# Zero-padded whole-array matmuls for attention and norms, and a reordered first stage, in a one-core encoder step

## The chip, the core and the metric

The kernel runs on one core of a Trainium2 chip. The metric is device time in microseconds (us): the median of three runs, and beside it one profiled execution, whose trace all rows below come from. The engines are called as the profile calls them: PE multiplies matrices (PEld is its weight load), DVE, ACT and POOL work elementwise, SP only issues transfers; ACT and POOL issue some too.

## The reference, cut to what matters

One layer for T = 320 positions (256 of a prompt, 64 of a running stream), model width 2048, everything in float32:

```python
z = rmsnorm(x) @ w_in                       # 2048 -> 3328: q 1024, k 128, v 128, gate input 2048
q, k = rmsnorm(q, q_g), rmsnorm(k, k_g)     # 16 query heads of 64, 2 key/value heads of 64
s = q @ k.T / 8 + bias                      # chunk of 64 queries against up to 192 keys
w = exp(s - m) / (sum(exp(s - m)) + exp(sink - m))
attn = w @ v
sgu = u * (W_s @ rmsnorm(v2) + b)           # u, v2 = gelu of the gate input; blocks of 128 positions
x = x + concat(rmsnorm(attn), rmsnorm(sgu)) @ w_out            # 2048 x 2048
y = x + square(relu(rmsnorm(x) @ w_up)) @ w_down               # 2048 x 8192 and back
```

## The kernel before, in words

Everything is held transposed: channels on the 128 partitions, the 320 positions along the free axis. The four large products run through `products` (L98): a weight block of 4 x 128 rows and 256 columns is loaded by SP into `w_raw` (the first stage into `w_first`), ACT rounds it into `w_hi` (L115), DVE takes the rest into `w_lo` (L116), and PE runs three passes per 128 x 128 piece, XH·w_hi, XL·w_hi and XH·w_lo (L125), each one instruction of 128x320. There are 8160 such instructions, called products from here on. `w_hi` and `w_lo` have two buffers each.

Between them stand the small float32 matmuls, each of which is two PE instructions (a transpose is one). `rstd_rows` (L136) sums squares over partitions into row form, three matmuls, the third for 64 positions; `spread` (L150) brings them back over 128 partitions. The first stage (L183) makes k, v and the first 256 columns of q, 192 products; `load_x` brings in x as it goes. Then the k norm is applied, `kq` holds keys times the gain, and `ksw` the same with the two key heads' partitions exchanged by two transfers from POOL. `attend(unit)` (L283) works on 64 queries and half of the heads' partitions, `hs`: four score matmuls of 64 rows into `s_ps` (L290), bias, softmax, four or eight transposes through `ident` (L321), and value matmuls with 64 output columns (L329). The gate group is mixed in L384 and L385, the latter with 64 rows. `bias` is built at the start: `tab` times `oneh` (L199) makes a row, which goes to DRAM as `b_dram` (L204) and comes back in 16 transfers (L212).

The order on each engine is set by a scheduler that simulates the program when it is built; each engine then works strictly in that order. The 192nd product ends the first stage; products are numbered along PE's order. PE's attention work stands between the 338th and 974th product.

Of the kernel before, what the change touches and what calls it, by code (L numbers as in the profile page):

```python
# [15 lines left out]
T = 320  # L16
TT = [(0, 128), (128, 128), (256, 64)]
# [11 lines left out]
def hymba_step_kernel(ctx: ExitStack, tc: tile.TileContext, i, o):  # L29
# [32 lines left out]
    nc.scalar.dma_start(out=xT[:, 0:1], in_=xv[:, 0:1])  # L62
# [29 lines left out]

    def chunks(n, first):
        if first:
            return [(0, 1), (1, 1), (2, 2)] + [(a, 4) for a in range(4, n, 4)]
        return [(a, 4) for a in range(0, n, 4)]

    def products(w, k0, nk, jobs, rh, rl, first=None, deep=None):  # L98
# [3 lines left out]
        for a, n in chunks(nk, first is not None):  # L102
# [4 lines left out]
            for j, (c0, ps) in enumerate(jobs):  # L107
# [6 lines left out]
                nc.sync.dma_start(out=raw[:, :n], in_=wv[:, k0 + a:k0 + a + n, c0:c0 + 256])  # L114
# [6 lines left out]
                for (k, g), (w_, r_, x) in [(kg, p_) for p_ in passes for kg in kgs] if first is not None else \  # L121
                        [(kg, p_) for kg in kgs for p_ in passes]:
                    kk = a + k
                    out = ps[g][:, 0:T] if isinstance(ps, list) else ps[:, g, 0:T]
                    nc.tensor.matmul(out=out, lhsT=w_[:, k, g * P:(g + 1) * P], rhs=r_(kk),  # L125
                                     start=(kk == 0 and x == 0), stop=(kk == nk - 1 and x == 2))
# [9 lines left out]
    def rstd_rows(sq, weight, eps, h=1):  # L136

        st = misc()
        for t, (t0, n) in enumerate(TT):
            nc.tensor.matmul(out=st[0:n, t * h:t * h + h], lhsT=sq[:, t0:t0 + n], rhs=weight, start=True, stop=True)  # L140
        r = sm.tile([P, 3 * h], F32, name="r_rows", tag="r_rows")
        nc.vector.memset(r[HD:P, 2 * h:3 * h], 1.0)
        nc.vector.tensor_scalar(out=r[:, 0:2 * h], in0=st[:, 0:2 * h], scalar1=eps, scalar2=None, op0=ALU.add)
        nc.vector.tensor_scalar(out=r[0:HD, 2 * h:3 * h], in0=st[0:HD, 2 * h:3 * h], scalar1=eps, scalar2=None,
                                op0=ALU.add)
# [30 lines left out]
    kq = at.tile([P, 448], F32, name="kq", bufs=1)  # L176
    ksw = at.tile([P, 448], F32, name="ksw", bufs=1)
# [43 lines left out]
    ssq = sm.tile([P, T], F32, name="ssq", tag="ssq", bufs=2)  # L221
    nc.vector.tensor_tensor(out=ssq, in0=ssq2[:, 0], in1=ssq2[:, 1], op=ALU.add)
# [7 lines left out]
    sq = sm.tile([P, T], F32, name="ksq", tag="w1", bufs=3)  # L230
    nc.scalar.activation(out=sq, in_=zk, func=AF.Square)
# [5 lines left out]
    for t, (t0, n) in enumerate(TT):  # L237
        nc.tensor.matmul(out=bc[:, t0:t0 + n], lhsT=rkx[0:n, t], rhs=ident[0:n, 0:n], start=True, stop=True)
    for dst, c in ((kn[:, 0:256], slice(0, 256)), (kn[:, 384:448], slice(256, 320))):
        nc.vector.scalar_tensor_tensor(out=dst, in0=zk[:, c], scalar=g_k, in1=bc[:, c], op0=ALU.mult, op1=ALU.mult)  # L240
    nc.vector.tensor_scalar(out=kq, in0=kn, scalar1=g_q, scalar2=None, op0=ALU.mult)
    nc.gpsimd.dma_start(out=ksw[0:HD], in_=kq[HD:P])
    nc.gpsimd.dma_start(out=ksw[HD:P], in_=kq[0:HD])
# [14 lines left out]
    for g in range(4):  # L258
# [16 lines left out]

    blocks = [
        (0, 0, 64, 128, None, vn[0]),
        (64, 0, 128, 64, vn[0], None),
        (128, 0, 192, 0, vn[0], vn[2]),
        (192, 64, 192, 0, vn[1], vn[3]),  # L280
        (256, 256, 192, 0, vC, vn[4]),
    ]
    def attend(unit):  # L283
        q0, k0, nk, b0, va, vb = blocks[unit // 2]
        p = unit % 2
        hs = slice(p * HD, (p + 1) * HD)
        s_ps = ps_sc.tile([P, 4, 256], F32, name="s_ps", tag="s_ps")
# [4 lines left out]
        s = at.tile([P, 4, 192], F32, name="s", tag="s", bufs=2)  # L292
        for j in range(4):
            c = 2 * (unit // 2) + p
            nc.vector.scalar_tensor_tensor(out=s[:, j, 0:nk], in0=s_ps[:, j, 0:nk], scalar=rq[:, j, c:c + 1],
                                           in1=bias[:, p, j, b0:b0 + nk], op0=ALU.mult, op1=ALU.add)
        m = at.tile([P, 4], F32, name="m", tag="m")
        nc.vector.tensor_reduce(out=m, in_=s[:, :, 0:nk], axis=AX.X, op=ALU.max)
        sk = sinks[:, 4 * p:4 * p + 4]
        nc.vector.tensor_tensor(out=m, in0=m, in1=sk, op=ALU.max)  # L300
        nm = at.tile([P, 4], F32, name="nm", tag="nm")
        nc.vector.tensor_scalar(out=nm, in0=m, scalar1=-1.0, scalar2=None, op0=ALU.mult)
        es = at.tile([P, 4], F32, name="es", tag="es")
        nc.vector.tensor_tensor(out=es, in0=sk, in1=m, op=ALU.subtract)
        nc.scalar.activation(out=es, in_=es, func=AF.Exp)
        den = at.tile([P, 4], F32, name="den", tag="den")
        for j in range(4):
            nc.scalar.activation(out=s[:, j, 0:nk], in_=s[:, j, 0:nk], func=AF.Exp, bias=nm[:, j:j + 1],
                                 accum_out=den[:, j:j + 1])
        nc.vector.tensor_tensor(out=den, in0=den, in1=es, op=ALU.add)  # L310
        nc.vector.reciprocal(out=den, in_=den)
        nc.gpsimd.tensor_tensor(out=s[:, :, 0:nk], in0=s[:, :, 0:nk],
                                in1=den[:, :, None].to_broadcast([P, 4, nk]), op=ALU.mult)
        parts = []
        c = 0
        for part, v, n in (("a", va, 128), ("b", vb, 64)):
            if v is None:
                continue
            pt_ps = misc()
            for j in range(4):  # L320
                nc.tensor.transpose(out=pt_ps[0:n, j * P:(j + 1) * P], in_=s[:, j, c:c + n], identity=ident)  # L321
            pt = at.tile([P, 512], F32, name="pt" + part, tag="pt" + part, bufs=1)
            nc.vector.tensor_copy(out=pt[0:n], in_=pt_ps[0:n])
            parts.append((pt, v, n))
            c += n
        for kv in range(2):
            o_ps = misc()
            for x, (pt, v, n) in enumerate(parts):
                nc.tensor.matmul(out=o_ps[hs, 0:256], lhsT=v[0:n, kv * HD:(kv + 1) * HD],  # L329
                                 rhs=pt[0:n, kv * 256:(kv + 1) * 256],  # L330
                                 start=(x == 0), stop=(x == len(parts) - 1))
            nc.scalar.activation(out=ao[hs, 4 * kv:4 * kv + 4, q0:q0 + 64],
# [190 lines left out]
```

## Time and profile before

| | |
|---|---|
| median of 3 runs | 1282.88 us (1282.8 to 1282.99) |
| profiled execution | 1281.25 us, span 1279.4 us |
| PE busy | 1272.5 us of the span (99%) |
| PEld, DVE, ACT, POOL busy | 1248.2, 635.2, 492.8, 101.4 us |
| DMA engines, mean rate over the span | 146 GB/s |

The span reaches from the first to the last instruction; the rest of the profiled time lies outside it. A matmul's end is modelled and includes its way through the array, so successive matmuls overlap in the trace; the distance between their starts is what PE spends on one.

### The profile page before, as it was taken

Reading aid. Unit: us, or ns where it says so; the run is one execution under the profiler, and the core shown is the slowest. Engines: PE = TensorE matmul, PEld = TensorE weight load, DVE = VectorE, ACT = ScalarE, POOL = GpSimd, SP = SyncE. Lnnn points to the kernel's source line nnn. Section 1 sums busy time; section 2 is a strip of 40 time slices with the busy share of each in tenths; the row PEclk is TensorE's granted clock in tenths of the full one; section 3 lists DMA queues with packets and bytes.
Section 4 is the critical chain, followed back from the end, with each engine's and each line's share of the span. In section 5 each row is a group of like instructions: output and inputs, shape, how many; then the busy total and the mean of one; then the engine's idle time right before and its main releaser. Section 6 shows DMA issues by size and latency. Waiting matters only on the chain.

```text
span 1279.4 us, 20199 instructions
## 1 busy us (share of the span) xinstructions
PE 1272.5 (99%) x8559; PEld 1248.2 (98%) x8559; DVE 635.2 (50%) x740; ACT 492.8 (39%) x644; POOL 101.4 (8%) x89
## 2 busy tenths in 40 slices
PE   8999999999999999999999999999999999999998
PEld 8999878999999999999999999999999999999998
DVE  7436765665774444343444444344443444444333
ACT  7325556432553433333334322233433323343222
POOL 0123335220230000000000000000000000000000
PEclk9999999999999999999999999999999999999999
DMA  9543323554454444445554444544444455544550
GB/s 301 150 128 99 99 83 100 175 162 149 149 150 147 149 148 149 149 150 149 153 152 154 149 149 149 149 149 149 149 151 152 149 153 151 150 148 159 169 169 32
DMA packets 186459, 187.79 MB, mean 147 GB/s; under 512 B 6400, under 2 KB 185904, under 8 KB 186368
## 3 DMA queue, kind: packets, MB, share of 16 engines
q1 hardware_dynamic: 185504, 185.17, 46.8%
q8 instruction: 67, 1.10, 0.4%
q0 software_dynamic: 432, 0.97, 0.3%
q10 hardware_dynamic: 432, 0.36, 0.1%
q14 instruction: 24, 0.20, 0.0%
HBM read 182.91 MB, written 3.32 MB: 146 GB/s over the span
## 4 chain that ended last, share of the span: by engine, by line
PE 99%; DMA 0%; ACT 0%; issue 0%; DVE 0%; POOL 0%; DVEq 0%; POOLq 0%; ACTq 0%
PE acc L125 92%; PE misc L329 1%; PE misc L125 1%; PE s_ps L290 1%; PE q_ps L125 1%; PE misc L321 1%; PE misc L269 0%; DMA tab<-in_table 0%; PE misc L384 0%; PE misc L140 0%; PE misc L154 0%; PE misc L385 0%; PE misc L376 0%; ACT sq L219 0%; PE misc L199 0%
## 5 line engine op out<-in xcount | busy, mean ns | idle before, releaser
L116 DVE TENSOR_TENSOR w_lo<-w_raw,w_hi 128x1024 fp32r<-128x1024 f32 x332 | 413.9, 1247 | 455.9 <-ACT w_hi L115 438.2
L115 ACT ACTIVATE w_hi<-w_raw 128x1024 fp32r<-128x1024 f32 x332 | 352.1, 1061 | 733.9 <-PE acc L125 684.9
L125 PE MATMUL acc<-H2H,w_lo 128*128 128x320 f32 x1024 | 316.6, 309 | 0.0
L125 PE MATMUL acc<-H2L,w_hi 128*128 128x320 f32 x1024 | 316.4, 309 | 0.0
L125 PE MATMUL acc<-H2H,w_hi 128*128 128x320 f32 x1024 | 316.4, 309 | 0.0
L125 PE MATMUL acc<-FH,w_hi 128*128 128x320 f32 x992 | 306.5, 309 | 0.0
L125 PE MATMUL acc<-FL,w_hi 128*128 128x320 f32 x992 | 306.5, 309 | 0.0
L125 PE MATMUL acc<-FH,w_lo 128*128 128x320 f32 x992 | 306.5, 309 | 0.0
L125 PEld LDWEIGHTS acc<-H2H,w_lo 128*128 128x128 f32 x1024 | 192.2, 188 | 0.1
L125 PEld LDWEIGHTS acc<-H2H,w_hi 128*128 128x128 f32 x1024 | 192.2, 188 | 0.0
L125 PEld LDWEIGHTS acc<-H2L,w_hi 128*128 128x128 f32 x1024 | 192.2, 188 | 0.0
L125 PEld LDWEIGHTS acc<-FH,w_hi 128*128 128x128 f32 x992 | 186.2, 188 | 0.0
L125 PEld LDWEIGHTS acc<-FL,w_hi 128*128 128x128 f32 x992 | 186.2, 188 | 0.0
L125 PEld LDWEIGHTS acc<-FH,w_lo 128*128 128x128 f32 x992 | 186.2, 188 | 0.0
L125 PE MATMUL acc<-XH,w_lo 128*128 128x320 f32 x384 | 117.8, 318 | 0.0
L125 PE MATMUL acc<-XH,w_hi 128*128 128x320 f32 x384 | 117.3, 317 | 0.2 <-ACT w_hi L115 0.2
L125 PE MATMUL acc<-XL,w_hi 128*128 128x320 f32 x384 | 116.1, 313 | 0.0
L125 PEld LDWEIGHTS acc<-XH,w_lo 128*128 128x128 f32 x384 | 71.5, 189 | 4.3 <-issue 3.1
L125 PEld LDWEIGHTS acc<-XH,w_hi 128*128 128x128 f32 x384 | 71.5, 189 | 3.9 <-issue 2.1
L125 PEld LDWEIGHTS acc<-XL,w_hi 128*128 128x128 f32 x384 | 71.6, 189 | 1.6 <-issue 1.4
L440 DVE SCALAR_TENSOR_TENSOR tf<-acc,r 128x640 f32<-128x640 f32 x32 | 26.4, 825 | 43.6 <-PE acc L125 43.6
L454 DVE TENSOR_TENSOR xT<-xT,acc 128x640 f32<-128x640 f32 x31 | 25.5, 821 | 41.8 <-PE acc L125 41.8
(173 smaller groups left out, 1033.8 us busy)
## 6 DMA issues: line engine op xcount, KB each, us to landing
w_raw<-in_w_up SPq DMA_DIRECT2D x128, 512.0 KB
w_raw<-in_w_down SPq DMA_DIRECT2D x128, 512.0 KB
w_raw<-in_w_in SPq DMA_DIRECT2D x44, 512.0 KB
w_raw<-in_w_out SPq DMA_DIRECT2D x32, 512.0 KB
w_first<-in_w_in SPq DMA_DIRECT2D x6, 512.0 KB
out_yT<-xT SPq DMA_DIRECT2D x7, 320.0 KB
xT<-in_xT SPq DMA_DIRECT2D x3, 640.0 KB
bias<-b_dram SPq DMA_DIRECT2D x16, 48.0 KB
```

The lines of the kernel that those rows point to most:

```text
L115: nc.scalar.activation(out=hi[:, :n], in_=raw[:, :n], func=AF.Copy)
L116: nc.vector.tensor_tensor(out=lo[:, :n], in0=raw[:, :n], in1=hi[:, :n].bitcast(F32), op=ALU.subtract)
L125: nc.tensor.matmul(out=out, lhsT=w_[:, k, g * P:(g + 1) * P], rhs=r_(kk), start=(kk == 0 and x == 0), stop=(kk == nk - 1 and x == 2))
L290: nc.tensor.matmul(out=s_ps[:, j, 0:nk], lhsT=qT[hs, q0 // 64, 2 * j:2 * j + 2].rearrange("p a t -> p (a t)"), rhs=keys[hs, k0:k0 + nk], s ...
L321: nc.tensor.transpose(out=pt_ps[0:n, j * P:(j + 1) * P], in_=s[:, j, c:c + n], identity=ident)
L329: nc.tensor.matmul(out=o_ps[hs, 0:256], lhsT=v[0:n, kv * HD:(kv + 1) * HD], rhs=pt[0:n, kv * 256:(kv + 1) * 256], start=(x == 0), stop=(x ...
L440: nc.vector.scalar_tensor_tensor(out=t, in0=ps[:, :, 0:T], scalar=0.0, in1=r2[:, None, :].to_broadcast([P, 2, T]), op0=ALU.max, op1=ALU.mult)
L454: nc.vector.tensor_tensor(out=xT[:, a:a + n], in0=xT[:, a:a + n], in1=p, op=ALU.add)
```

## The change

What the parts of the diff do:

- The table product L199 (L221 after) is ordered behind the last product of the first stage (`issue_after`), and the 16 `bias` transfers go from SP's queue to POOL's.
- x's first block moves from ACT's queue to the head of SP's, and all weight and x loads on SP are chained in program order.
- Scores: keys lie in `kz`, 128 rows of which 64 are zero, once for each half; one matmul of all 128 rows gives both halves' scores side by side. A unit is now 64 queries and one key head.
- Values lie in `vz` between two blocks of 64 zero columns, so that a slice of 128 columns puts one half's result on its partitions and adds zero on the others. Keys are cut 96 + 96 where they were 128 + 64.
- Row sums run over 384 positions, the last 64 zero; `spread`, `rkx` and L385 take all 128 rows.

```diff
-    nc.scalar.dma_start(out=xT[:, 0:1], in_=xv[:, 0:1])
...
+    def load(out, in_):
+        with tc.issue_after(loads[-1].ins) if loads else nullcontext():
+            loads.append(nc.sync.dma_start(out=out, in_=in_))
...
-        for t, (t0, n) in enumerate(TT):
-            nc.tensor.matmul(out=st[0:n, t * h:t * h + h], lhsT=sq[:, t0:t0 + n], rhs=weight, start=True, stop=True)
+        for t in range(3):
+            nc.tensor.matmul(out=st[:, t * h:t * h + h], lhsT=sq[:, t * P:(t + 1) * P], rhs=weight, start=True, stop=True)
...
-            nc.tensor.matmul(out=bc[:, t0:t0 + n], lhsT=rs[0:n, t:t + 1].to_broadcast([n, P]),
-                             rhs=ident[0:n, 0:n], start=True, stop=True)
+            nc.tensor.matmul(out=bc[:, t0:t0 + n], lhsT=rs[:, t:t + 1].to_broadcast([P, P]),
+                             rhs=ident[:, 0:n], start=True, stop=True)
...
-    nc.tensor.matmul(out=b_ps[0:16, 0:255], lhsT=tab, rhs=oneh, start=True, stop=True)
+    with tc.issue_after(mm.ins):
+        nc.tensor.matmul(out=b_ps[0:16, 0:255], lhsT=tab, rhs=oneh, start=True, stop=True)
...
-                nc.sync.dma_start(out=bias[hh * HD:(hh + 1) * HD, p, j], in_=src)
+                nc.gpsimd.dma_start(out=bias[hh * HD:(hh + 1) * HD, p, j], in_=src)
...
-        (192, 64, 192, 0, vn[1], vn[3]),
+        (192, 64, 192, 0, [(vn[64], 96), (vn[160], 96)]),
...
-        for j in range(4):
-            keys = kq if j // 2 == p else ksw
-            nc.tensor.matmul(out=s_ps[:, j, 0:nk], lhsT=qT[hs, q0 // 64, 2 * j:2 * j + 2].rearrange("p a t -> p (a t)"),
-                             rhs=keys[hs, k0:k0 + nk], start=True, stop=True)
+        for j in range(2):
+            a = 2 * (2 * kv + j)
+            nc.tensor.matmul(out=s_ps[:, j, 0:2 * nk].rearrange("x (p k) -> x p k", p=2),
+                             lhsT=qT[:, blk_, a:a + 2].rearrange("p a t -> p (a t)"),
+                             rhs=kz[:, kv, :, k0:k0 + nk], start=True, stop=True)
...
-                nc.tensor.matmul(out=o_ps[hs, 0:256], lhsT=v[0:n, kv * HD:(kv + 1) * HD],
-                                 rhs=pt[0:n, kv * 256:(kv + 1) * 256],
+                nc.tensor.matmul(out=o_ps[:, 0:256], lhsT=v[0:n, kv, HD - p * HD:3 * HD - p * HD],
+                                 rhs=pt[0:n, p * 256:(p + 1) * 256],
...
-        nc.tensor.matmul(out=sp_ps[:, 256:T], lhsT=vnat_s[:, cs], rhs=wsT[0:HD, g, 0:HD], start=True, stop=True)
+        nc.tensor.matmul(out=sp_ps[:, 256:T], lhsT=vnat_s[:, cs], rhs=wsT[:, g, 0:HD], start=True, stop=True)
```

**How rows move.** First the start of PE's order (`acc` is the sum for k and v, `q_ps` that for q), before and then after:

```order
L78 MATMUL misc<-idle 128x256 x3
L199 MATMUL misc<-oneh,tab 16x255
L125 MATMUL acc<-XH,w_hi 128x320 x2
L125 MATMUL q_ps<-XH,w_hi 128x320 x2
L125 MATMUL acc<-XL,w_hi 128x320 x2
```
```order
L78 MATMUL misc<-idle 128x256 x3
L132 MATMUL acc<-XH,w_hi 128x320 x2
L132 MATMUL acc<-XL,w_hi 128x320 x2
L132 MATMUL acc<-XH,w_lo 128x320 x2
L132 MATMUL q_ps<-XH,w_hi 128x320 x2
```

The table product is gone from the front (it follows the 192nd product), and k and v take their three passes before q begins. Next ACT at the same place, from the first block of x up to the first weight block of 4 x 128 rows (128x1024), before and after; 128x256 and 128x512 are the blocks of rows 0 to 1 and 2 to 3:

```order
L162 ACTIVATE XH<-xT,cols 128x320 x2
L219 ACTIVATE sq_453<-xT 128x640
L115 ACTIVATE w_hi<-w_first 128x256 x2
L115 ACTIVATE w_hi<-w_first 128x512
L162 ACTIVATE XH<-xT,cols 128x320 x2
L115 ACTIVATE w_hi<-w_first 128x512
L162 ACTIVATE XH<-xT,cols 128x320 x2
L219 ACTIVATE sq_456<-xT 128x640
L219 ACTIVATE sq_459<-xT 128x640
L115 ACTIVATE w_hi<-w_first 128x1024 x2
```
```order
L122 ACTIVATE w_hi<-w_first 128x256
L173 ACTIVATE XH<-xT,cols 128x320
L237 ACTIVATE ssq_455<-xT 128x640
L122 ACTIVATE w_hi<-w_first 128x256 x2
L173 ACTIVATE XH<-xT,cols 128x320 x2
L240 ACTIVATE sq_457<-xT 128x640
L122 ACTIVATE w_hi<-w_first 128x256
L122 ACTIVATE w_hi<-w_first 128x512 x2
L173 ACTIVATE XH<-xT,cols 128x320 x4
L240 ACTIVATE sq_460<-xT 128x640
L240 ACTIVATE sq_463<-xT 128x640
L122 ACTIVATE w_hi<-w_first 128x1024 x2
```

All four XH and both squares now stand between the second 128x512 block and the first 128x1024 one. Then PE in attention, value matmuls followed by the next unit's scores for a chunk with 192 keys, before and after:

```order
L329 MATMUL misc<-ptb,v_64_537 64x256
L329 MATMUL misc<-pta,v_128_529 64x256
L329 MATMUL misc<-ptb,v_64_537 64x256
L290 MATMUL s_ps<-ksw,qT 128x192 x2
L290 MATMUL s_ps<-kq,qT 128x192 x2
L125 MATMUL acc<-XH,w_lo 128x320
```
```order
L132 MATMUL acc<-XH,w_lo 128x320
L363 MATMUL misc<-pt_1270,vz 128x256 x2
L354 MATMUL misc<-ident,s 96x128 x4
L318 MATMUL s_ps<-kz,qT 128x384 x2
L132 MATMUL acc<-XH,w_hi 128x320
```

Four scores of 192 columns became two of 384, and value matmuls have 128 output rows instead of 64. Last POOL, from the row to DRAM up to the exchange of the key heads (`rs_rows` is the power -1/2 in `rstd_rows`; the one of 128x3 is x's, that of 128x6 is k's), before and after:

```order
L204 DMA b_dram<-b_row 240x1x255
L195 MEMSET wsT 64x8x64
L147 TENSOR_TENSOR rs_rows<-r_rows,nhalf 128x3
L246 DMA out_vpT<-vT 128x128
L247 DMA out_vsT<-vT 128x64
L147 TENSOR_TENSOR rs_rows<-r_rows,nhalf 128x6
L244 DMA out_kpT<-kn 128x128
L245 DMA out_ksT<-kn 128x64
L242 DMA ksw<-kq 64x448
L243 DMA ksw<-kq 64x448
```
```order
L225 DMA b_dram<-b_row 240x1x255
L158 TENSOR_TENSOR rs_rows<-r_rows,nhalf 128x3
L233 DMA bias<-b_dram 64x1x192 x16
L270 DMA out_vpT<-vT 128x128
L271 DMA out_vsT<-vT 128x64
L139 MEMSET acc_s 128x64
L158 TENSOR_TENSOR rs_rows<-r_rows,nhalf 128x6
L268 DMA out_kpT<-kn 128x128
L269 DMA out_ksT<-kn 128x64
L266 DMA kz<-kz 64x448
L267 DMA kz<-kz 64x448
```

All 16 bias transfers stand on POOL between x's power and k's. PE's matmul that spreads k's factors (`rkx`, L238 and L260) moves from behind the 290th product to behind the 378th, the first score from the 338th to the 432nd, and the last value matmul from the 974th to the 898th. Outside the products PE has 226 matmuls after, 246 before.

## Rows read from the trace of the kernel before

**Rows 1.** The page: busy time of PE and the chain that ended last, by engine and by line.
```profile
PE 1272.5 (99%) x8559; PEld 1248.2 (98%) x8559; DVE 635.2 (50%) x740; ACT 492.8 (39%) x644; POOL 101.4 (8%) x89
PE 99%; DMA 0%; ACT 0%; issue 0%; DVE 0%; POOL 0%; DVEq 0%; POOLq 0%; ACTq 0%
```

**Rows 2.** A stretch table (length, then busy time of each engine, granted clock, DMA share, GB/s) from the end of the first stage to the last small matmul, and the piece of the chain that follows it (start, us, instructions).
```profile
38.28:385.51 347.23, 347.23 (x2292) 325.33 (x2290) 221.10 (x340) 156.20 (x290) 98.30 (x79) 1.00 0.44 133
...
385.51 876.38 PE acc L125 x5974
```

**Rows 3.** PE in order of time (start, us), value matmuls of a chunk with 192 keys, with products ahead and behind.
```profile
158.14 0.31 PE L125 MATMUL acc<-XH,w_hi 128*128 128x320 f32 x1
158.38 0.65 PE L329 MATMUL misc<-pta,v 128*64 128x256 f32 x2
...
159.21 0.31 PE L125 MATMUL acc<-XH,w_lo 128*128 128x320 f32 x1
...
160.67 0.31 PE L125 MATMUL acc<-XH,w_hi 128*128 128x320 f32 x1
160.91 0.64 PE L329 MATMUL misc<-ptb,v 64*64 64x256 f32 x2
...
162.63 0.42 PE L125 MATMUL acc<-XL,w_hi 128*128 128x320 f32 x1
162.88 0.31 PE L125 MATMUL acc<-XH,w_lo 128*128 128x320 f32 x1
```

**Rows 4.** The same view, scores of 64 rows and then transposes of the whole array.
```profile
150.16 0.31 PE L125 MATMUL acc<-XH,w_lo 128*128 128x320 f32 x1
150.39 0.91 PE L290 MATMUL s_ps<-ksw,qT 64*128 64x192 f32 x4
151.15 0.81 PE L290 MATMUL s_ps<-kq,qT 64*128 64x192 f32 x4
151.89 0.42 PE L125 MATMUL acc<-XH,w_hi 128*128 128x320 f32 x1
152.14 0.31 PE L125 MATMUL acc<-XL,w_hi 128*128 128x320 f32 x1
...
154.04 0.31 PE L125 MATMUL acc<-XH,w_lo 128*128 128x320 f32 x1
154.19 1.03 PE L321 MATMUL misc<-ident,s 128*128 128x128 f32 x8
154.98 0.39 PE L125 MATMUL acc<-XH,w_hi 128*128 128x320 f32 x1
155.21 0.31 PE L125 MATMUL acc<-XL,w_hi 128*128 128x320 f32 x1
```

**Rows 5.** The chain (start, us, instructions) where the gate group is mixed, then a row sum of the whole array (four instructions of one column).
```profile
228.50 0.44 PE misc L384 x4
228.95 0.36 PE misc L385 x2
229.31 0.64 PE acc L125 x3
...
249.75 0.34 PE misc L140 x4
```

**Rows 6.** PE and then ACT in order of time at the start; in brackets the idle time before, and what ended it.
```profile
6.21 1.00 PE L199 MATMUL misc<-oneh,tab 32*16 32x255 f32 x2 [2.00 <-DMA tab<-in_table]
7.14 0.90 PE L125 MATMUL acc<-XH,w_hi 128*128 128x320 f32 x2
...
12.11 0.66 PE L125 MATMUL q_ps<-XL,w_hi 128*128 128x320 f32 x2
12.61 0.47 PE L125 MATMUL acc<-XH,w_lo 128*128 128x320 f32 x2
...
17.06 0.70 PE L125 MATMUL acc<-XH,w_hi 128*128 128x320 f32 x3 [0.17 <-ACT w_hi L115]
...
4.50 0.56 ACT L162 ACTIVATE XH<-xT,cols 128x320 fp32r<-128x320 f32 x1 [0.87 <-DMA cols<-in_cols]
4.97 0.71 ACT L115 ACTIVATE w_hi<-w_first 128x256 fp32r<-128x256 f32 x2
6.48 0.56 ACT L162 ACTIVATE XH<-xT,cols 128x320 fp32r<-128x320 f32 x1 [0.81 <-DMA xT<-in_xT]
...
14.69 1.36 ACT L219 ACTIVATE sq<-xT 128x640 f32<-128x640 f32 x2
15.95 2.00 ACT L115 ACTIVATE w_hi<-w_first 128x1024 fp32r<-128x1024 f32 x2
```

**Rows 7.** POOL in order of time (k's power, then the exchange of the key heads), between them PE's spreading of k's factors, and from the table of transfers (KB each, us from issue to landing) those of POOL that matter here.
```profile
50.90 1.35 POOL L147 TENSOR_TENSOR rs_rows<-r_rows,nhalf 128x6 f32<-128x6 f32 x1 [2.53 <-DVE r_rows L144]
...
55.14 0.97 PE L238 MATMUL misc<-ident,rkx 128*128 128x128 f32 x6
...
58.81 0.54 POOL L242 DMA_DIRECT2D ksw<-kq  x1 [0.74 <-DVE kq L241]
59.34 0.52 POOL L243 DMA_DIRECT2D ksw<-kq  x1
...
b_dram<-b_row POOLq DMA_DIRECT2D x1, 239.1 KB, 8.0
ksw<-kq POOLq DMA_DIRECT2D x2, 112.0 KB, 4.1
```

More of the change, by code (lines that the diff above doesn't have):

```diff
@@ L124, in products, with sums @@
                     out = ps[g][:, 0:T] if isinstance(ps, list) else ps[:, g, 0:T]
-                    nc.tensor.matmul(out=out, lhsT=w_[:, k, g * P:(g + 1) * P], rhs=r_(kk),
-                                     start=(kk == 0 and x == 0), stop=(kk == nk - 1 and x == 2))
+                    mm = nc.tensor.matmul(out=out, lhsT=w_[:, k, g * P:(g + 1) * P], rhs=r_(kk),
+                                          start=(kk == 0 and x == 0), stop=(kk == nk - 1 and x == 2))
+        return mm
+    def sums(name):
+        t = sm.tile([P, TP], F32, name=name, tag="ssq", bufs=2)
+        nc.gpsimd.memset(t[:, T:TP], 0.0)
+        return t
     def acc_tile():
@@ L182, in hymba_step_kernel @@
     q0_ps = ps_sc.tile([P, 2, 512], F32, name="q0_ps", tag="s_ps")
-    products(w_in, 0, KT, [(1024, kv_ps), (0, q0_ps)], xh, xl, first=load_x)
+    mm = products(w_in, 0, KT, [(1024, kv_ps), (0, q0_ps)], xh, xl, first=load_x)
     nc.sync.dma_start(out=kn[:, 256:384], in_=i["ckT"])
-    vC = at.tile([P, P], F32, name="vC", bufs=1)
-    nc.sync.dma_start(out=vC, in_=i["cv"])
+    kz = blk("kz", [P, 2, 2, 448])
+    for h in range(2):
+        nc.gpsimd.memset(kz[HD:P, h, 0], 0.0)
+        nc.gpsimd.memset(kz[0:HD, h, 1], 0.0)
+    vz = blk("vz", [P, 6, 2, 3 * HD])
+    nc.gpsimd.memset(vz, 0.0)
+    cv = i["cv"].rearrange("k (h d) -> k h d", h=2)
+    vC = vz[:, 5]
+    nc.gpsimd.dma_start(out=vC[0:96, :, HD:P], in_=cv[0:96])
     sinks = at.tile([P, 8], F32, name="sinks", bufs=1)
@@ L220, in hymba_step_kernel @@
         nc.vector.tensor_tensor(out=ssq2, in0=ssq2, in1=sq, op=ALU.add)
[L221 to L222 removed]
+    ssq = sums("ssq")
+    nc.vector.tensor_tensor(out=ssq[:, 0:T], in0=ssq2[:, 0], in1=ssq2[:, 1], op=ALU.add)
     rx = spread(rstd_rows(ssq, inv_dm, EPS), "rx")
@@ L293, in attend @@
[L293 to L299, printed above, removed]
+        blk_, kv = unit // 2, unit % 2
+        q0, k0, nk, b0, parts = blocks[blk_]
@@ new lines, in attend @@
+        if nk < P:
+            nc.gpsimd.memset(s[:, :, :, nk:P], 0.0)
+        for p in range(2):
+            for j in range(2):
+                c = 2 * blk_ + p
+                nc.vector.scalar_tensor_tensor(out=s[:, p, j, 0:nk], in0=s_ps[:, j, p * nk:(p + 1) * nk],
+                                               scalar=rq[:, 2 * kv + j, c:c + 1],
+                                               in1=bias[:, p, 2 * kv + j, b0:b0 + nk], op0=ALU.mult, op1=ALU.add)
+        m = at.tile([P, 2, 2], F32, name="m", tag="m")
@@ L304, in attend @@
         nc.vector.tensor_tensor(out=es, in0=sk, in1=m, op=ALU.subtract)
         nc.scalar.activation(out=es, in_=es, func=AF.Exp)
[L306 to L309, printed above, removed]
+        den = at.tile([P, 2, 2], F32, name="den", tag="den")
+        for p in range(2):
+            for j in range(2):
+                nc.scalar.activation(out=s[:, p, j, 0:nk], in_=s[:, p, j, 0:nk], func=AF.Exp, bias=nm[:, p, j:j + 1],
+                                     accum_out=den[:, p, j:j + 1])
@@ new lines, in attend @@
+        for x, (pt, (v, n)) in enumerate(zip(pts, parts)):
+            for p in range(2):
+                nc.tensor.matmul(out=o_ps[:, 0:256], lhsT=v[0:n, kv, HD - p * HD:3 * HD - p * HD],
+                                 rhs=pt[0:n, p * 256:(p + 1) * 256],
+                                 start=(x == 0 and p == 0), stop=(x == len(parts) - 1 and p == 1))
+        nc.scalar.activation(out=ao[:, 4 * kv:4 * kv + 4, q0:q0 + 64],
+                             in_=o_ps[:, 0:256].rearrange("p (a q) -> p a q", a=4), func=AF.Copy)
```

110 lines of the change are left out of this document (53 added, 57 removed).

## The prediction

> **What bounds the kernel now.** The page first: PE is busy for 99% of the span, the next engine for half of it, and 99% of the chain that ended last is PE [rows 1]. A shorter time can only come from fewer microseconds of PE, or from an earlier start. The stretch table and the chain then say what PE's time is made of. Behind the last small matmul 5974 products take 876.38 us, 0.1467 each [rows 2]. In the stretch from the first stage's end (38.28) to 385.51 lie 1898 products (the 193rd to the 2090th), 278.4 us at that price; the stretch is 347.2 us long and PE is busy in all of it [rows 2], so the small matmuls cost **68.8 us**. None of PE's idle time lies there, and no other engine is waited for. Ahead of 38.28 PE idles 2.0 us for the small table `tab`, spends 1.0 on its product, and waits once more, 0.17 us, for ACT [rows 6].
>
> Next the timeline, for what a small matmul costs: the distance from the last product before a group to the second product behind it, less two steps of 0.147. A value matmul pair alone: 158.14 to 159.21, less 0.29, is 0.78; three in a row 1.92 (160.67 to 162.88) [rows 3]. Inside, an instruction takes 0.287 (1.72 / 6), and the edges together cost 0.20. Scores: 150.16 to 152.14 gives 1.69, of which 1.50 inside, 0.1875 per instruction of 192 columns [rows 4]. Groups that use the whole array are cheaper at both points. Eight transposes cost 0.88 (154.04 to 155.21), with edges of 0.09 and so 0.099 each with them, 0.088 without [rows 4]. An instruction of 128 columns takes 0.11 (0.44 / 4), one of a single column 0.085 (0.34 / 4), while L385's 64 columns through 64 rows take 0.18 each (0.36 / 2), and the three products behind them 0.64 where three steps are 0.44: an edge of 0.20 again [rows 5].
>
> **The change part by part.** *Small matmuls.* After it each of them is a whole-array one, except the table product. I price the new order by count:
>
> - scores, 40 instructions: 8 of 128 columns at 0.11, 8 of 256 and 24 of 384. The last two widths have no whole-array row at full speed; in proportion to 0.11 they are 0.22 and 0.33. Together 10.6.
> - values, 64 instructions of 256 columns at 0.22: 14.1. Both are the same number of columns as before; what goes is the half-array surcharge, 0.287 to 0.22 and 0.1875 to 0.165 for 192 columns.
> - transposes, 93 at 0.088: 8.2.
> - gate group, 32 of 128 columns at 0.11 and 16 of 64 columns at 0.10 (between 0.085 and 0.11): 5.1. Before, the 16 alone cost 16 x 0.18 + 8 x 0.20 = 4.5; now 1.6.
> - `spread` and k's factors, 20 of 128 columns and 10 of 64: 3.2.
> - row sums, 36 of one or two columns at 0.09: 3.2; q's sums, unchanged, 40 at 0.10: 4.0.
> - edges: the order after has 63 groups between products, at 0.09 each: 5.7.
>
> Sum 54.1, against 68.8: **-14.7 us**. Bounds: the wide ones can't be cheaper than the 128-column row without its part that does not grow; if all of 0.005 is fixed, 0.215 and 0.32, the sum falls by 0.6. On the dear side a wide one costs at most what the half-array one does, which is a rival below.
>
> *Table product.* It now runs behind the first stage at full speed. Its 32 rows make it a partial one; the nearest row is the value pair, 0.78 [rows 3]. **+0.8**, between 0.3 (two whole-array instructions of 0.085 and an edge) and 1.0 (its own old row [rows 6]).
>
> *Start.* Today the first product starts at 7.14, right behind the table product, though XH and the first `w_hi` were there at 5.33 (4.97 + 0.36) [rows 6]. XH itself waited for `cols`, which ACT now issues first instead of second; I take 4.95 for the first product, 2.2 us earlier. Not all of it lasts. Up to 12.1 products start 0.267 apart, 320 columns at 1.2 GHz, and from 12.6 about 0.147 apart [rows 6], though the profile's clock row for that stretch says full speed throughout. In the new order k and v take six products (to 6.55), then q's `w_hi` stands on ACT behind the second XH and a square. The second block of x landed at 6.48 [rows 6]; issued some 0.45 earlier, it lands at about 6.0, and 0.47 + 0.63 + 0.36 of ACT later q may go on at 7.45. Sixteen products behind that, q's pass with XL over the second block ends and frees the buffer for the second 128x512 `w_hi`: at 11.1 if full speed comes 2 us earlier than today (11 slow, 5 fast), at 11.7 if not. Behind that `w_hi` (0.55, between 0.36 and the 1.0 of one four times as large) stand four XH (1.9, by the pace of 0.47), two squares (1.26) and the 128x1024 `w_hi` (1.0) [rows 6]: the first large block starts at 15.8 or 16.4, instead of 17.06. If speed comes still earlier (from about 9), 14.9. From there 144 products at 0.1467 run to the stage's end, as today (17.06 to 38.28). I take 15.8, **-1.3**, with -2.2 and -0.7 as ends.
>
> *Transfers.* Weights were never waited for by PE behind 17 us [rows 2, 6], so the chained order gains nothing. Its cost would be the `bias` transfers, now on POOL, a rival below.
>
> **Sum.** -14.7 + 0.8 - 1.3 = -15.2 on the profiled execution's 1281.25, so 1266.05; the median stands 1.63 above that execution, so **1267.7 us**.
>
> **The rivals.**
> *1. The 96-wide pieces count as partial.* Six of ten units cut keys 96 + 96. If 96 rows pay the old price, 48 value instructions cost 0.067 more and 12 edges 0.11 more [rows 3]: +4.5, 1272.1. Against it: 96 is over half of the array, and no row has any piece between 64 and 128.
>
> *2. The new order stalls PE a little.* Scheduler and chip differ, and some distances are short. From the start of k's spread to the landing of the second key exchange were 55.14 to 59.34 + 4.1 = 63.4, 8.3 us [rows 7]; now PE wants it after the spread, 54 products and five transposes, some 9.4 us. On DVE a `w_lo` now stands behind the first biased scores, and these behind POOL's powers for q: a short distance too. I give each slip 1 to 3 us, of the size of such a distance; two make 1269 to 1273, centre 1271.
>
> *3. Width doesn't matter, only the columns and edges as they are.* The zeros add no useful work; if half-array instructions cost what they do for another reason than the half, scores and values keep their price and only start and table change: -0.5, 1282.4. Against it stand L384 and L385, 0.11 for 128 columns and 0.18 for 64 in one place [rows 5]. The Trainium skill (TensorE: Matmul & The Clock Gate, "Why this matters for your kernels") speaks for it: it has a matmul of few rows take the same time as one of 128, and would have small ones run side by side in separate row groups rather than padded. By that the small matmuls would gain nothing. No row here shows such running side by side: the eight score instructions follow one another at 0.1875 [rows 4].
>
> *4. Slower: POOL.* The 16 `bias` transfers stand ahead of k's power, that ahead of `rkx` on ACT, and behind `rkx` the `w_hi` of the 385th product. Stage end 37.0 (15.8 + 21.2), table, row copy: the row goes to DRAM at about 38; it landed after 8.0 us [rows 7], so 46. Sixteen at 0.54 (the exchange's issue, [rows 7]) end at 54.6; two outputs, the power (1.35 [rows 7]) and `rkx` reach 57.7. PE wants that `w_hi` at about 68.9 (38.4 behind table and row sums, 28.2 for 192 products, 2.3 of small ones), `rkx` 1.3 earlier: 9.9 us to spare. Each issue may take 0.54 + 9.9 / 16 = 1.16 before PE waits, and 2.1 before all of the 15 us is lost. If each waited for its own landing at 4.1 [rows 7], the stall would be 16 x 3.56 - 9.9 = 47 us: 1315. Against it: the two exchanges were issued 0.53 apart, not 4.1. The Trainium skill (SBUF — State Buffer, "SBUF: two separate sides") says that DVE, in one of its modes, locks POOL out of writing transfer descriptors; the 8.0 us of the row to DRAM, beside 4.1 for the exchange, would fit that, and by it this rival grows.
>
> **How the numbers follow.** The forecast holds with 0.70, rival 1 with 0.09, rival 2 with 0.13, rivals 3 and 4 with 0.04 each. The forecast's own range is 1265 to 1270: start and table give -1.4 to +0.8, the wide prices -0.6 to about +1 if they keep 0.01 more than in proportion. To hold eight in ten with rivals 1 and 2 mostly inside, the range is 1264 to 1273. A change of under 0.2% (2.6 us) is about what a measurement of this kernel can't tell from none. Faster: 0.70 + 0.09 + 0.13 = 0.92; same 0.04 (rival 3); slower 0.04 (rival 4).
>
> **What would show it.** In the changed profile the first product at about 5; the first 128x1024 block's at 15 to 16; the 192nd product's end near 37.0; value groups of four instructions at 0.22 with edges of 0.09; the stretch from the first stage's end to the last small matmul (385.51 today) about 333 us long; no idle time of PE behind 17 us. Value instructions near 0.29 in the chunks with 192 keys mean rival 1, gaps of PE between 50 and 110 us rival 2, at every score rival 3, and a gap that ends with POOL's power near the 378th product rival 4. What would make it wrong above all is a wait that no row of today shows, since every engine's order is new.

## The result, and the profile after

The changed kernel takes 1269.71 us, the median of four executions (1268.12 to 1269.81), against 1282.84 for the kernel before in the same session: ratio 0.9899, 95% interval 0.9881 to 0.9916. The forecast was 1267.7. The profiled execution took 1269.68 (span 1267.7), 11.6 less than the one of before, where 15.2 less was forecast.

The page of after gives PE's busy time and then its granted clock in 40 slices of the span, in tenths of full speed:

```profile
PE 1258.4 (99%) x8519; PEld 1249.4 (99%) x8519; DVE 639.8 (50%) x729; ACT 489.2 (39%) x634; POOL 119.4 (9%) x121
PEclk9989999999999999999999999999999999999999
```

PE is the bound as in [rows 1], but the third slice, from 63 to 95 us, has an 8. The chain (start, us, instructions) from the first stage's end to the last small matmul is the counterpart of [rows 2]:

```profile
36.89 0.53 PE misc L221 x2
37.42 0.76 PE misc L154 x6
...
49.08 0.56 PE misc L154 x6
...
66.91 0.61 PE misc L260 x6
...
373.85 876.24 PE acc L132 x5974
```

The stage ends 1.39 us earlier. The stretch from 36.89 to 373.85 is 336.96 long where it was 347.23, so 10.3 less; about 333 was forecast. The products behind it take as long as before. Inside the stretch, again from the chain:

```profile
77.89 2.13 PE misc L293 x20
80.02 2.18 PE acc L132 x11
82.20 1.93 PE misc L293 x10
84.13 5.81 PE acc L132 x27
...
94.19 1.01 PE misc L293 x10
...
95.70 3.95 PE acc L132 x27
99.65 0.86 PE misc L363 x4
...
106.08 0.44 PE misc L354 x4
...
112.65 1.29 PE s_ps L318 x4
...
134.81 0.87 PE misc L363 x4
...
211.48 0.17 PE misc L420 x2
```

L363 are values, L354 transposes, L318 scores, L293 q's row sums, and L420 is the 64-column matmul of the gate group. The 27 products from 84.13 are 0.215 apart on average, where the 27 from 95.70 are 0.146 apart, and ten of q's row sums take 1.93 at 82.20 and 1.01 at 94.19. The stretch table (length, busy time of each engine, granted clock, DMA share, GB/s) says why:

```profile
77.00:81.00 4.00, 4.00 (x35) 4.00 (x34) 1.54 (x3) 0.00 (x0) 1.80 (x1) 1.00 0.52 165
81.00:87.00 6.00, 6.00 (x27) 6.00 (x26) 2.45 (x7) 1.06 (x1) 4.06 (x3) 0.50 0.08 26
88.00:94.00 6.00, 6.00 (x44) 6.00 (x43) 2.21 (x5) 3.15 (x10) 1.45 (x1) 1.00 0.40 100
```

The clock was at its lower level, 1.2 GHz, for six to seven microseconds while the trace shows no gap of PE. Such a stretch is called a dip from here on. Against full speed the three pieces from 80.02 lost 0.57 + 0.92 + 1.85 = **3.3 us**. PE also waits; in order of time, with the idle time and what ended it in brackets:

```profile
171.70 0.42 PE L132 MATMUL acc<-XH,w_lo 128*128 128x320 f32 x1 [0.28 <-DVE w_lo L123]
...
198.82 0.41 PE L132 MATMUL acc<-XH,w_hi 128*128 128x320 f32 x1 [0.17 <-ACT w_hi L122]
...
199.75 0.63 PE L411 MATMUL misc<-ident,gv 128*64 128x128 f32 x4 [0.38 <-ACT vnat L413]
201.96 0.42 PE L132 MATMUL acc<-XH,w_lo 128*128 128x320 f32 x1 [1.58 <-DVE w_lo L123]
```

These waits are **2.4 us** in all. Ahead of the longest, ACT and then DVE did this:

```profile
192.80 3.73 ACT L173 ACTIVATE AH<-ao,cols 128x320 fp32r<-128x320 f32 x8
196.43 0.82 ACT L374 ACTIVATE sq<-ao 128x320 f32<-128x320 f32 x2
197.15 0.67 ACT L413 ACTIVATE vnat<-misc,rs_rows 128x512 f32<-128x512 f32 x1
197.72 1.05 ACT L122 ACTIVATE w_hi<-w_raw 128x1024 fp32r<-128x1024 f32 x1
...
196.99 3.78 DVE L174 SCALAR_TENSOR_TENSOR AL<-ao,cols,AH 128x320 fp32r<-128x320 f32 x4
200.69 1.21 DVE L123 TENSOR_TENSOR w_lo<-w_raw,w_hi 128x1024 fp32r<-128x1024 f32 x1
```

All eight splits of the attention output into a rounded part AH (on ACT) stand in one piece ahead of a weight's `w_hi`, and half of the rests AL (on DVE) ahead of its `w_lo`.

So the account of the profiled executions is: start -1.4, table +0.7 (0.53, and 0.20 that the row sums behind it take more than those at 49.08), waits +2.4, clock +3.3. For all other small matmuls this leaves 336.96 - 278.4 - 0.7 - 2.4 - 3.3 = 52.1 where they were 68.8, so -16.7; this last term is what is left over, and it takes up any error of the others. The sum is -11.7, against -11.6 measured.

### The profile page after: what moved, and what is told of

Read it like the earlier page. It is cut to its first block, busy times and chain, and to the rows that moved or that the text cites. A ratio compares the mean times of both kernels' runs of the same rounds, so it can differ in the third digit from the quotient of the medians.

```text
span 1267.7 us, 20131 instructions
## 1 busy us (share of the span) xinstructions
PE 1258.4 (99%) x8519; PEld 1249.4 (99%) x8519; DVE 639.8 (50%) x729; ACT 489.2 (39%) x634; POOL 119.4 (9%) x121
## 4 chain that ended last, share of the span: by engine, by line
PE 97%; ACT 1%; DMA 1%; DVE 0%; SPq 0%; POOL 0%; issue 0%; ACTq 0%; POOLq 0%
PE acc L132 91%; PE misc L132 1%; PE misc L363 1%; PE q_ps L132 1%; PE s_ps L318 1%; DMA xT<-in_xT 1%; PE misc L354 1%; PE misc L293 0%; DVE w_lo L123 0%; PE misc L419 0%; SPq L98 0%; PE misc L154 0%; ACT AH L173 0%; PE misc L165 0%; ACT w_hi L122 0%; ACT vnat L413 0%
```

## The experiments

The profiled execution gained 3.6 us less than forecast. Two theories were to be told apart: these went to the two new costs named above (clock and waits), each with its cause in one place; or the small matmuls gained less than priced, and the low clock comes by chance. Each execution also carries a mean granted clock, which is 1.000 where no dip is to be seen. The kernel before, run 46 times beside the experiments, shows what that is worth: its 20 executions at 1.000 took 1280.02 to 1281.58, its 26 below took 1281.92 to 1283.24.

**One cause each.** `wide_q` widens q's row sums:

```diff
-    hone = const.tile([P, 2], F32, name="hone")
+    hone = const.tile([P, 64], F32, name="hone")
-            nc.tensor.matmul(out=st[:, 2 * b:2 * b + 2], lhsT=sq[:, b].rearrange("p a t -> p (a t)"), rhs=hone,
+            nc.tensor.matmul(out=st[:, 64 * b:64 * b + 64], lhsT=sq[:, b].rearrange("p a t -> p (a t)"), rhs=hone,
```

> The changed kernel, with q's row sums widened: each of the 20 matmuls L293 now has 64 columns in place of 2 (the extra ones times zero), in the same order on every engine but for one product. Theory: the clock fell to 0.50 from 81.0 to 87.6 because PE did little work per instruction in the row sums around it; with 32 times the columns the granted clock stays at 1.00 there, the 3.3 us that products and sums lost come back, and the wider instructions cost 0 to 0.4: 1266.4 to 1266.8 us against 1269.7. Rival: the clock falls because small matmuls stand close together there, whatever their columns, or for a reason outside PE (no DMA moves anything from 82 to 88): the dip stays 6.6 us long and the time is 1269.7 to 1270.1.

Measured: 1268.24 (1266.52 to 1268.55). The dip is gone from its place, and another stands in and behind PE's waits, which begin near 196:

```profile
82.00:88.00 6.00, 6.00 (x46) 6.00 (x45) 3.58 (x11) 2.92 (x11) 3.44 (x2) 1.00 0.10 24
195.00:198.00 3.00, 2.00 (x13) 1.22 (x11) 3.00 (x4) 3.00 (x6) 2.44 (x4) 1.00 0.00 0
198.00:204.00 6.00, 4.86 (x24) 4.87 (x25) 3.78 (x4) 2.89 (x5) 4.27 (x2) 0.72 0.52 145
```

Only the one execution at 1.000, 1266.52, has the expected time; the other three were at 0.997 to 0.999. At the old place the DMA share was low here too (0.10, against 0.08 with the dip), so a low share alone does not lower the clock. `ah_late` leaves the sums as they are and spreads the splits over the four groups of u, half of the gate input (`his` collects the `w_hi` copies):

```diff
-            for a in range(8):
-                add_square(acc_a, ao[:, a], a == 0)
-                split(ao[:, a], g_oa[:, a:a + 1], AH[:, a], AL[:, a])
...
         u_ps = product(w_in, 0, KT, 1280 + g * 256, xh, xl)
+        for a in range(2 * g, 2 * g + 2):
+            with tc.issue_after(his[-3].ins):
+                add_square(acc_a, ao[:, a], a == 0)
+                split(ao[:, a], g_oa[:, a:a + 1], AH[:, a], AL[:, a])
```

> The changed kernel, with the eight AH splits and squares of the attention output issued two per u group, behind the second of that group's four w_hi on ACT, where before all eight AH stood in one row ahead of a w_hi. Theory: PE's waits at 198.8, 199.8 and 202.0 (0.17 + 0.38 + 1.58, and up to 0.5 around them) come from those 3.7 us of ACT in one piece; they go, the clock dip stays: 1267.1 to 1267.6 us. Rival: ACT and DVE are full there anyway (13.2 and 12.8 of 17 us busy), and the wait only turns up at the next w_hi: 1269.2 to 1269.9.

Measured: 1263.92 (1263.37 to 1266.62), three of four executions at 1.000, the fourth at 0.997. Here is the stretch of the waits, first in the changed kernel, then in this one:

```profile
186.00:203.00 17.00, 14.87 (x106) 14.09 (x105) 12.77 (x15) 13.17 (x24) 11.19 (x11) 1.00 0.27 82
```
```profile
186.00:203.00 17.00, 17.00 (x128) 16.93 (x128) 9.78 (x16) 11.26 (x17) 5.01 (x5) 1.00 0.51 141
```

The waits of this stretch are gone and did not come back later (the 0.28 stays, at 168). In three executions the dip went too, which the expectation had staying, although the two-column sums are untouched. Without dip and without these waits the stretch from the first stage's end to the last small matmul is 331.0 long, which leaves 51.6 for the small matmuls. `wide_ah` makes both edits.

> Both edits together: q's row sums with 64 columns and the AH splits spread over the u groups. Theory: the clock falls where PE does little, in the row sums (81 us) or in the wait (199 to 202 us); with both gone every execution shows a mean granted clock of 1.000 (0.9995 and up), the median is 1263.2 to 1264.2 us and none lies above 1265. Rival: the dips come by chance at any place of the first 370 us and one execution in four or more still has a clock of 0.997 to 0.999 and 1265 to 1267 us.

Measured: 1263.77, all four executions at 1.000 and within 0.2 us (1263.63 to 1263.81).

**Is it the two-column sums?** `before_wide` is the `wide_q` edit on the kernel before, `tiny2_ah` repeats each sum on `ah_late`:

> The kernel before, with q's 20 row-sum matmuls L269 of 64 columns in place of 2, and nothing else; the order on every engine is the same. 10 of 22 executions of the kernel before so far had a mean granted clock of 0.997 to 0.999 and lay 1 to 2 us above the others. Theory: the two-column sums bring the clock down; with 64 columns every execution is at 1.000 and between 1280.5 and 1282.2 us (0 to 0.4 for the columns). Rival: the dips have nothing to do with these sums; four in ten executions still show 0.997 to 0.999.

Measured: 1281.2, eleven executions from 1280.65 to 1281.69; two of them have 0.999 in the records, at 1281.34 and 1281.44, so not every one is at 1.000 as the theory had it. (Of the 22 executions of before that the expectation counts, 11, not 10, were below 1.000.) Beside it the kernel before ran to 1283.04, median 1282.21; the ratio, 0.9993 (0.9984 to 1.0002), does not tell the medians apart, but no execution lies in the upper group of times, from 1281.92.

```diff
+            nc.tensor.matmul(out=st[:, 64 + 2 * b:66 + 2 * b], lhsT=sq[:, b].rearrange("p a t -> p (a t)"), rhs=hone,
+                             start=True, stop=True)
```

> The kernel with spread AH splits, each of q's 20 two-column row sums done twice (the second into columns that nobody reads). 40 more PE instructions at 0.10: 4.0 us. Theory: more of the two-column work in one place lowers the clock in every execution, for 6.6 us or longer: 1263.9 + 4.0 + 3.3 = 1271.2 us or more, clock at most 0.997. Rival: the dip does not depend on them; one execution in four dips as without the second sums, median 1267.9.

Measured: 1274.48 (1272.58 to 1275.69), all five executions at 0.993 to 0.996. In the profiled one the lower level lasted 10 us:

```profile
82.00:93.00 11.00, 11.00 (x50) 11.00 (x50) 3.58 (x13) 2.59 (x10) 4.79 (x4) 0.53 0.00 1
```

The scheduler moved other rows of this kernel too, so not all of the 10.6 us above `ah_late` belong to the sums. Taken together: with wider sums there are fewer dips, with more sums a dip each time. The sums are not the whole cause: with the same sums the changed kernel dips in four executions of four and `ah_late` in one of four. What in them lowers the clock stays open.

**The parts of the change.** `start_only` puts the start, the table and the queues into the kernel before; `shapes_only` takes them out of the changed one. This is the core of the first edit; the second is the same the other way round:

```diff
-    nc.scalar.dma_start(out=xT[:, 0:1], in_=xv[:, 0:1])
+        with tc.issue_after(loads[-1].ins) if loads else nullcontext():
+            loads.append(nc.sync.dma_start(out=out, in_=in_))
+    with tc.issue_after(mm.ins):
         nc.tensor.matmul(out=b_ps[0:16, 0:255], lhsT=tab, rhs=oneh, start=True, stop=True)
-                nc.sync.dma_start(out=bias[hh * HD:(hh + 1) * HD, p, j], in_=src)
+                nc.gpsimd.dma_start(out=bias[hh * HD:(hh + 1) * HD, p, j], in_=src)
```

> The kernel before with the start alone changed: table product behind the 192nd product, first block of x on SP's queue, loads chained, bias transfers on POOL. All small matmuls as before. Theory: -1.4 at the start and +0.5 for the table: 1282.0 us against 1282.8 (1281.5 to 1282.4). Rival: the widths don't matter and the gain of 13 us came with the start and the queues: 1270 to 1275. Rival on the other side: moving the start brings a stall or a clock dip here too: 1283 to 1286.

> The changed kernel with its start undone: the table product ahead of the first product again, the first block of x on ACT's queue, the bias transfers on SP, loads not chained. What is left is the whole-array part. Theory: the parts add up, 1.4 us later at the start and 0.5 less behind the first stage: 1270.6 us (1270.2 to 1271.0). Rival: the clock dip or the waits hang on the order that the start sets, and without it they are gone: 1265 to 1268.

Measured: `start_only` 1284.03 (1281.19 to 1286.07), ratio 1.0014 (1.0005 to 1.0022). Its stage ends at 37.28, 1.0 earlier, but the stretch behind is 0.86 longer, 0.72 of it the table and its edge:

```profile
37.28 0.53 PE misc L207 x2
37.81 0.74 PE misc L147 x6
...
385.37 876.38 PE acc L131 x5974
```

The last small matmul ends 0.14 earlier than in [rows 2]. At a clock of 1.000 its times, 1281.19 to 1281.41, lie among those of before (1280.02 to 1281.58); eight of eleven executions are below 1.000, down to 0.995, and that makes its median the worse one.

`shapes_only` took 1271.84 (1270.32 to 1272.53), 0.9922 of before and 9.7 us less in its session: the whole-array matmuls alone give most of the 13.1 us. That is above what was expected, and the rival fell too, for the waits around 200 us stay. PE also waits 1.03 and 0.70 at 242 and 243 for a `w_hi` and its `w_lo`, which the changed kernel does not: without the chain the last block of `w_in` was issued at 234.46, behind eight blocks of `w_out`, and the DMA engines were full (share 1.10 and more) up to 241. All five executions are below 1.000, and the profiled one dips twice, once in and behind the waits (0.66 from 201 to 206), and once directly behind its 20 two-column sums, here at another time and again without a gap of PE (the chain, then the stretch table):

```profile
65.71 2.13 PE misc L292 x20
...
65.00:70.00 5.00, 5.00 (x36) 5.00 (x36) 0.82 (x4) 1.06 (x1) 2.99 (x2) 0.86 0.36 105
70.00:75.00 5.00, 5.00 (x29) 5.00 (x29) 3.08 (x8) 1.24 (x2) 0.92 (x1) 0.80 0.39 105
```

**The price of a partial matmul.** A partial matmul is one that uses only part of the array's rows. Both edits are made on `ah_late`. `cut_ah` cuts keys 128 + 64, and `norms_ah` gives row sums, `spread`, `rkx` and L420 their 64 rows back:

```diff
-        (192, 64, 192, 0, [(vn[64], 96), (vn[160], 96)]),
+        (192, 64, 192, 0, [(vn[64], 128), (vn[192], 64)]),
```

> The kernel with spread AH splits, its 192 keys cut 128 + 64 in place of 96 + 96 (values and transposes; the order on every engine is the same). 24 value instructions then have 64 rows. Theory: a half-array instruction of 256 columns costs 0.287 for 0.216 and its group's edges 0.20 for 0.09: 24 x 0.071 + 6 x 0.11 = 2.4 us longer from the first stage's end to the last small matmul (331.0 before this edit, 333.4 with it), 1266.3 us. Rival: only columns and edges count: 331.0 and 1263.9.

Measured: the stretch is 332.5 long where `ah_late` has 331.0 with its 0.28 of waiting at 168, which is missing here: 1.8 more, where 2.4 were expected. The one execution at a clock of 1.000 took 1265.58; the other three, at 0.996 and 0.997, put the median at 1268.53. The first two lines are values of 64 rows and the transposes behind them, the other two are transposes and values of 128 rows:

```profile
134.29 1.06 PE misc L362 x4
135.35 0.59 PE misc L353 x4
...
139.42 0.44 PE misc L353 x4
...
140.01 0.86 PE misc L362 x4
```

The partial group takes 0.20 more and the next one 0.15: up to 0.35 a group. Six groups would be 2.1 by that, a little more than was measured.

```diff
-            nc.tensor.matmul(out=bc[:, t0:t0 + n], lhsT=rs[:, t:t + 1].to_broadcast([P, P]),
-                             rhs=ident[:, 0:n], start=True, stop=True)
+            nc.tensor.matmul(out=bc[:, t0:t0 + n], lhsT=rs[0:n, t:t + 1].to_broadcast([n, P]),
+                             rhs=ident[0:n, 0:n], start=True, stop=True)
-        nc.tensor.matmul(out=sp_ps[:, 256:T], lhsT=vnat_s[:, cs], rhs=wsT[:, g, 0:HD], start=True, stop=True)
+        nc.tensor.matmul(out=sp_ps[:, 256:T], lhsT=vnat_s[0:HD, cs], rhs=wsT[0:HD, g, 0:HD], start=True, stop=True)
```

> The kernel with spread AH splits, in which row sums, spread, k's factors and L420 have 64 rows again in their last part (as in the kernel before); scores and values stay whole-array. Theory: L420's 16 instructions cost 0.18 for 0.085 and 8 edges 0.11 more (2.4 us), five spreads 0.20 each more (1.0), row sums nothing: the stretch from the first stage's end to the last small matmul grows from 331.0 to 334.4, 1267.3 us. Rival: such short ones cost what they did, and all of the gain is in scores and values: 331.0 to 331.5, 1263.9 to 1264.4.

Measured: 1268.8 (1268.54 to 1268.87 at a clock of 1.000), the stretch 335.7: 4.7 more, where 3.4 were expected. The gate group takes 2.7 of them (L420 is L423 here, and L419, its 128-column matmul, is L422) and the spreads 1.0:

```profile
202.70 0.36 PE misc L423 x2
203.06 0.64 PE misc L422 x4
203.70 0.36 PE misc L423 x2
```

The 64-row pair takes 0.36 where it took 0.17, and the whole-array four behind it 0.64 for 0.50. These two runs change the rows at an equal number of instructions. Scores were not undone alone: there half as many instructions, each twice as wide, came with the full array, and no run tells the two apart.

**What the start and the queues hide.** `sq_ah` adds to `ah_late`:

```diff
-        nc.scalar.activation(out=sq, in_=xT[:, k:k + 2], func=AF.Square)
+        with tc.issue_after(his[min(7 + 2 * (k // 4), len(his) - 1)].ins):
+            nc.scalar.activation(out=sq, in_=xT[:, k:k + 2], func=AF.Square)
```

> The kernel with spread AH splits, and the squares of x issued on ACT behind the w_hi of the first 128x1024 blocks, where two of them stood ahead of the first one (1.36 us on the chain of the changed kernel). Theory: the first 128x1024 product starts 1.2 us earlier, at 14.1 to 14.4, the 192nd product ends near 35.5, 1262.7 us. Rival: the stage is bound by its transfers (DMA share 1.06 to 1.09 from 9 to 16 us): PE waits the same time at the next block, 1263.9. Rival on the other side: x's row sums come late and PE waits for them behind 37 us: 1264 to 1266.

Measured: 1263.45; the two executions at a clock of 1.000 took 1262.27 and 1262.69, the other two are at 0.999 and 0.997. The first 128x1024 block starts at 14.08 and the stage ends at 35.46, both 1.18 earlier than in `ah_late`: the squares on ACT held that start. The four XH ahead of it wait for x's transfer here (0.58), so that the transfers come next. `sq_wide_ah` has all three edits:

> All three edits on the changed kernel: q's row sums with 64 columns, AH splits spread over the u groups, squares of x behind the first w_hi of 128x1024. Theory: the edits add up and no execution loses its clock (all 1.000): 1263.77 less the 1.2 of the squares, 1262.2 to 1262.8 us with a spread under 1. Rival: as without the wide sums two executions in four show 0.997 to 0.999 and 1264 to 1266.

Measured: 1262.64 (1262.22 to 1262.74), one execution at 0.999 and not slower, the others at 1.000; the ratio to the kernel before is 0.9848 (0.9835 to 0.9862), and the time lies 7.1 us below the changed kernel's median. `queues_undone` takes the chain of loads out of it and puts the `bias` transfers back on SP:

```diff
-        with tc.issue_after(loads[-1].ins) if loads else nullcontext():
-            loads.append(nc.sync.dma_start(out=out, in_=in_))
+        nc.sync.dma_start(out=out, in_=in_)
-                nc.gpsimd.dma_start(out=bias[hh * HD:(hh + 1) * HD, p, j], in_=src)
+                nc.sync.dma_start(out=bias[hh * HD:(hh + 1) * HD, p, j], in_=src)
```

> The kernel with all three edits, the queue part of the change undone: loads no longer chained (w_out's first eight blocks then go ahead of the last three of w_in), the 16 bias transfers on SP again, behind the fifth w_raw. Theory: PE never waits for a weight behind 17 us in either order, so the queues gain and cost nothing: 1262.2 to 1263.0 us. Rival: the 16 issues on SP, 0.4 to 0.5 each, hold the weights behind them for 7 us and PE waits for one, or a chain helped: 1264 to 1270. Rival on the other side: POOL, free of the 16 issues, gives k's power sooner and the earlier order of k's matmuls saves a wait: under 1262.

Measured: 1270.36 (1270.13 to 1273.07). The theory falls. Here is first SP in order of time, then PE where it waited:

```profile
42.81 10.05 SPq L232 DMA_DIRECT2D bias<-b_dram  x16
52.96 6.73 SPq L97 DMA_DIRECT2D w_raw<-in_w_in  x4
...
220.54 7.51 SPq L97 DMA_DIRECT2D w_raw<-in_w_out  x5
228.16 2.45 SPq L97 DMA_DIRECT2D w_raw<-in_w_in  x2
```
```profile
58.09 0.42 PE L131 MATMUL acc<-XH,w_hi 128*128 128x320 f32 x1 [0.81 <-ACT w_hi L121]
59.35 0.41 PE L131 MATMUL acc<-XH,w_lo 128*128 128x320 f32 x1 [0.70 <-DVE w_lo L122]
...
237.35 0.41 PE L131 MATMUL acc<-XH,w_hi 128*128 128x320 f32 x1 [3.01 <-ACT w_hi L121]
238.61 0.64 PE L131 MATMUL acc<-XH,w_lo 128*128 128x320 f32 x1 [0.70 <-DVE w_lo L122]
```

With the table product behind the first stage the bias row comes back when SP should load weights, and its transfers held them for 10 us. The sixth block of weights was issued only at 52.96, and PE waits 1.5 us for what is made of it and of the next. Without the chain five blocks of `w_out` went ahead of the last two of `w_in`, whose landing PE then awaited, 3.7 us in all. Behind the second wait the clock is low (0.61 from 238.6 to 243).

## Why the prediction was right, and where not

- **The sum's direction and size** held: 1269.7 lies in the range, 2.0 above the forecast. It lies in the forecast's own range (1265 to 1270) and in that of rival 2 (1269 to 1273) too, so the number alone does not tell them apart; the traces show something of both.
- **Start** (forecast -1.3, measured -1.4). The first product starts at 5.03 (4.95 was forecast), the first 128x1024 block at 15.51 (15.8), and the 192nd product ends at 36.89 (37.0). XH, two squares and `w_hi` on ACT were the right chain, as `sq_ah` shows. What led up to it was not: products stand 0.147 apart from about 9.3 us on (0.267 ahead of that), some 3 us earlier than before, which is the case for which the prediction had 14.9 (by its own steps it is 15.2). The second 128x512 `w_hi` began at 10.49 instead of 11.1, and the four XH then waited for x's transfer, on which the prediction had no term:

```profile
11.32 1.93 ACT L173 ACTIVATE XH<-xT,cols 128x320 fp32r<-128x320 f32 x4 [0.20 <-DMA xT<-in_xT]
```

  That the start came so close is in part luck.
- **Table** (forecast +0.8, measured +0.7). Start, table and queues together are worth nothing that can be measured on the kernel before, by `start_only`.
- **Small matmuls** (forecast -14.7, measured -16.7). The wide instructions cost what was said or a little less: values 0.215 (0.86 / 4), scores 0.3225 for 384 columns (1.29 / 4), the 64-column ones 0.085 (0.17 / 2, priced 0.10). The transposes were misread: [rows 4] have eight of them in 0.79, and 0.88 with the edges, so 0.099 and 0.11 each, where the sum took 0.088; after, they take 0.11 (0.44 / 4), which for 93 is 2 us more than the sum had. The term that was mis-sized is the edges, 5.7 us for 63 groups. Almost all of them lie inside the groups' own time: 27 products right behind four transposes take 3.95, which is 27 steps of 0.146, and 0.86 and 1.29 are no more than the price of the columns. That outweighs the transposes: 52.1 is left where 54.1 was summed.
- **"No idle time of PE behind 17 us"** was wrong by 2.4 us. That is the mechanism of rival 2, the scheduler's order against the chip's times, but at 171 and 199 us and through ACT's pieces, not at the two short distances that were named.
- **The clock** was in no term and in no rival, and cost 3.3 us. The prediction took products at 0.147 behind the start because before's profiled execution has 1.00 throughout [rows 2]; more than half of before's executions do not.
- **Luck.** Waits and clock were 5.7 too cheap and the small matmuls 2.0 too dear, so the profiled execution missed by 3.6. The median missed by only 2.0, because the forecast added the 1.63 by which before's median stood above its profiled execution. After has no such distance (1269.71 and 1269.68). Before's median of three carries no clock, but its executions lie where those with a dip do, so the 1.63 is most likely the price of a dip: the forecast held half of the clock's cost without knowing it.
- **"The chained order gains nothing"** was right against before and wrong of the new order: chain and POOL together keep 7.7 us away there, by `queues_undone` against `sq_wide_ah`. Of these, 1.5 are waits behind the bias row, which the table's move brings about, and 3.7 are waits from the order of the loads, of which `shapes_only` has 1.7; most of the rest is the low clock behind them.
- **Rivals.** 1 (96 rows count as partial) is false: four values take 0.86 with 128 rows (at 99.65) and 0.87 with 96 (at 134.81). 3 is false: `shapes_only` takes 0.9922 of before's time with the whole-array part alone. The Trainium skill (TensorE: Matmul & The Clock Gate, "Why this matters for your kernels") gives a matmul of few rows the time of one of 128; here 64 rows cost more, 0.36 for 0.17 in L420, and the measurement decides. 4 (POOL) is false: k's factors are spread at 66.91 without a wait, the row landed in DRAM after 5.1 us, and 15 of the 16 transfers were issued in 8.49 us, 0.57 each, as the prediction had it.

## What to carry over

Where PE is the bound, count the groups of matmuls that don't fill the array: in the two runs that put 64 rows back, each cost 0.2 to 0.35 us, and zero padding took that away at no price on PE. Read the mean clock of every execution before you compare medians, and where it falls, look at what PE did just ahead: here it was a run of two-column matmuls or a wait. After a change that moves rows, look on each engine for one long piece of work ahead of a weight's preparation. Undo the parts that "gain nothing" once more on the new order: they may be what keeps it going.

## What was not expected of the hardware

- The clock fell to its lower level with no gap of PE in the trace (busy 6.00 of 6.00 us, clock 0.50), behind 20 PE instructions of two columns; `shapes_only` shows it at another place. By the mean clocks it happens in some executions of a kernel and not in others. The Trainium skill (TensorE: Matmul & The Clock Gate, "Why this matters for your kernels") names idle gaps of PE for drops in mid-kernel; the dips behind waits (0.72 at 198 to 204 in `wide_q`, 0.61 behind 238.6 in `queues_undone`) lie in that direction, this one does not.
- 62 more columns cost a row sum almost nothing: ten instructions of 64 columns take 1.06 in `wide_q` (at 82.21), ten of two columns take 1.01 in the changed kernel (at 94.19).
